# A hybrid RWKV-7 / Fourier layer on one core: four blocks normalised inside the scan, modulation weights loaded in another order, eight pairs of Fourier tiles

## The chip, the cores and the metric

The kernel runs on one core of a Trainium2 chip. The metric is the device time of one execution in microseconds; lower is better. Before the change the median of three runs is 3580.61 us (3576.83 to 3589.69).

## What is computed

One transformer-like layer over 2048 latent tokens of width 1024, with 256 context tokens ahead of them. In short (float32 throughout):

```
mod  = silu(c) @ w_ada + b_ada                  (shift, scale, gate; also for c_ctx)
h    = rmsnorm(x) * (1 + scale) + shift
p    = h @ w_in                                 (RWKV columns | Fourier columns | gates)
y_f, y_b = RWKV-7 scans of p over the tokens, forward and backward (context first)
o    = groupnorm_by_head(y_f + y_b) * lnx_g + lnx_b + bonus * v
r    = (o * (sigmoid(gd) @ g2)) @ w_up_r
f    = real(DFT over grid and channels) @ w_up_f
x1   = x + ga1 * ((sigmoid(gate_f) * f + sigmoid(gate_r) * r) @ w_out)
out  = rmsnorm(x1 + ga2 * swiglu(modulated rmsnorm(x1)))
```

## The kernel before

The work is in stages that follow one another. Large products are made of three single products of split operands (`hi*hi + hi*lo + lo*hi`, `mm3`, lines 251 to 253), 128x128 weights against 512 tokens.

**Modulation (lines 166 to 218).** Shift and scale of the first norm come from sixteen weight tiles of 512 KB: `wk` (line 197, TensorE products `modps` for the shift) and `wr` (line 190, VectorE products with `sB` and `sC`, the broadcast silu(c) and silu(c_ctx), summed into `mod`; `mod_j1` is the one for the context). `wk` and `wr` have three buffers each. `sB` and `sC` are loaded first. Then a loop over the eight k scales the first 512 latent tokens (`scaled`), and at once adds the shift and splits the result into `hh` and `hl` (`moved`), first for one half of the tokens, then for the other; three `mod_j1` stand in it. TensorE starts the first products of `w_in` (`pxps`, `fps`) on each k as it comes.

**Input projection (to about 1000 us)**, bound by TensorE.

**Scan (to 1776 us).** A loop over turns s from -2 to 17, each of 128 tokens in both directions. Its order is written out by hand: instructions given through the handles `PE, DV, AC, GP, SY` stay in program order on their queues. A turn inverts small triangular matrices on VectorE for the coming turns (`invert`), passes them through memory (`inv_store`, `merge_load`), merges their halves (`merge_a`: VectorE transposes `T` and TensorE `wps`; `merge_b`: VectorE `Wb`; `merge_c`: TensorE `t21ps`, ScalarE `TT`), and runs two links of the recurrence (`Chain`: `x`, `u`, `z`, `state`, `y`). At seven places in a turn `fill()` takes one step of a generator that supplies other work: first late gate columns, then `fourier()`. Its second part makes `fm = f @ w_up_f`: 32 steps of 12 products `pf`, 512 tokens in each `tb` (order 1, 2, 0, 3), against four pairs of tiles `fh`, `fl` loaded from memory (`load_f`). There are seven pairs in a ring: of the next `tb` three pairs are loaded ahead, the fourth when its buffer is free, at the first step of that `tb`. Once in a turn `ahead` loads weights `wf` and these tiles.

After `pf` the generator opens a pool for the group normalisation (`gn_open`, with the weights `g2`) and runs `gn_steps` for the four blocks of 128 tokens of the first `tb`. Each block goes through five steps: load of `y`, `yb`, `v` and the gate columns `sg`; sum of both directions, mean and centring (VectorE) and a square (ScalarE); variance, square root (ScalarE) and scaling; four transposes `gnt` (TensorE), four ScalarE evictions, addition of `v`; product `gng` with `g2` and multiplication. The `fill()`s of the loop are used up when this begins, so the blocks are worked off after the last turn.

**Merge and output product (1776 to about 2200 us).** `c_merge(n)` (lines 1135 to 1160) splits the four normalised blocks into `oh` and `ol`, makes `pr` (eight column tiles, 12 products each, weights `wr`), multiplies with the gates `gr` and adds `gf * fm`. These three operands of 256 KB for each column tile come from memory into a ring of eight buffers `t2`. For n > 0 `c_merge` normalises its own blocks (`gn_block`). Its instructions carry no fixed order: the compiler's planner places them. The order is merge 0, merge 1, output product `po` of 0, merge 2, and so on. `po` takes the weights `w_out` through `load_w`.

**Feed-forward (2200 us to the end)**, bound by TensorE.

## Time and profile before

| | |
|---|---|
| median of 3 runs | 3580.61 us |
| the profiled execution's own time | 3583.36 us |
| its span, first to last instruction | 3581.5 us |
| TensorE busy (products) | 3271.8 us, 91% |
| VectorE busy | 2405.0 us, 67% |
| ScalarE busy | 1560.3 us, 44% |
| GpSimd busy | 701.3 us, 20% |
| mean granted TensorE clock | 0.948 of full speed |

The span is the time from the first to the last instruction in the trace. Busy time is the time in which an engine had an instruction under way. The granted clock is the share of TensorE's full clock that it was given: 1.00 is 2.4 GHz, 0.50 is 1.2 GHz. A row of the timeline gives start and duration in us, engine, line (line 59 is the helper behind the handles of fixed order), operation, output and inputs, and in brackets how long the engine had been idle and what ended the wait. SPq is the queue of SyncE, which issues most transfers.

### The profile page before, as it was taken

The page shows a single profiled execution, that of the slowest core. Times are in us where ns is not written, and L with a number is a line of the kernel's source. Part 1 is how long each engine was busy: PE and PEld are TensorE (multiplying, and loading weights), DVE is VectorE, ACT ScalarE, POOL GpSimd, SP SyncE. Part 2 cuts the span into 40 slices and gives each one's busy share as a digit, 9 for nine tenths or more (in the row PEclk, how much of TensorE's full clock was granted, in tenths as well). Part 3 has the DMA queues.
Part 4 walks back from the last instruction along what each step waited for, and adds up shares of the span by engine and source line. Part 5 has one row for each costly group of instructions (what it writes and reads, how often), then busy time and mean ns, then how long its engine had stood idle before and what let it go on. Part 6 is the DMA issues. An engine that isn't in the chain of part 4 may idle for free.

```text
span 3581.5 us, 56320 instructions
## 1 busy us (share of the span) xinstructions
PE 3271.8 (91%) x20574; PEld 2700.2 (75%) x20574; DVE 2405.0 (67%) x4467; ACT 1560.3 (44%) x2910; POOL 701.3 (20%) x1099
## 2 busy tenths in 40 slices
PE   6999899999988887998758898999998999999997
PEld 5787777877877776777646686888877878888876
DVE  6677678757557777666376669777775387776354
ACT  3667556657543444434433335333353333333332
POOL 1143332322223333212132322000020000000000
PEclk9999999999999887999869998999999999999998
DMA  5354655545445556676677655222264432222453
GB/s 196 108 171 156 206 194 174 183 128 164 150 166 151 161 172 194 197 216 191 188 258 237 234 185 165 92 83 86 80 199 156 147 106 85 82 84 87 159 172 101
DMA packets 308436, 561.01 MB, mean 157 GB/s; under 512 B 91296, under 2 KB 102816, under 8 KB 308160
## 3 DMA queue, kind: packets, MB, share of 16 engines
q1 hardware_dynamic: 264256, 418.29, 36.4%
q0 software_dynamic: 43904, 139.12, 12.0%
q8 instruction: 163, 2.67, 0.3%
q14 instruction: 113, 0.93, 0.1%
HBM read 405.62 MB, written 151.66 MB: 156 GB/s over the span
## 4 chain that ended last, share of the span: by engine, by line
PE 36%; issue 10%; DVE 6%; DMA 6%; ACT 1%; POOL 1%; SPq 0%; DVEq 0%; POOLq 0%; ACTq 0%
PE pd L1352 12%; PE pT L251 2%; PE pT L252 2%; PE pT L253 2%; PE pf L59 2%; PE pB L251 2%; PE pB L252 2%; PE pB L253 2%; PE po L253 1%; PE po L251 1%; PE po L252 1%; PE xr L59 1%; DMA gr<-g_dr 1%; PE qk L59 1%; DMA wraw<-w_down 1%
## 5 line engine op out<-in xcount | busy, mean ns | idle before, releaser
L245 DVE TENSOR_TENSOR wlo<-wraw,whi 128x512 fp32r<-128x512 f32 x462 | 310.0, 695 | 378.3 <-ACT whi L244 365.6
L244 ACT ACTIVATE whi<-wraw 128x512 fp32r<-128x512 f32 x462 | 276.9, 626 | 483.9 <-PE pd L1352 192.7
L1352 PE MATMUL pd<-uh,whi 128*128 128x512 f32 x704 | 278.4, 396 | 23.1 <-ACT whi L244 21.5
L1352 PE MATMUL pd<-ul,whi 128*128 128x512 f32 x704 | 276.8, 393 | 0.0
L251 PE MATMUL pxps<-hh,whi 128*128 128x512 f32 (+2 forms) x720 | 252.1, 351 | 16.8 <-ACT hh L152 10.7
L1352 PE MATMUL pd<-uh,wlo 128*128 128x512 f32 x704 | 254.1, 391 | 0.7 <-DVE wlo L245 0.7
L251 PE MATMUL fps<-hh,whi 128*128 128x512 f32 (+1 forms) x688 | 249.2, 362 | 0.1
L252 PE MATMUL pxps<-hl,whi 128*128 128x512 f32 (+2 forms) x720 | 248.1, 346 | 0.0
L253 PE MATMUL pxps<-hh,wlo 128*128 128x512 f32 (+2 forms) x720 | 245.7, 346 | 2.4 <-DVE wlo L245 2.2
L253 PE MATMUL fps<-hh,wlo 128*128 128x512 f32 (+1 forms) x688 | 245.6, 357 | 1.4 <-DVE wlo L245 1.4
L252 PE MATMUL fps<-hl,whi 128*128 128x512 f32 (+1 forms) x688 | 243.6, 354 | 0.0
L1290 DVE TENSOR_TENSOR u<-u,pT 128x512 f32<-128x512 f32 x176 | 120.9, 687 | 142.0 <-PE pT L253 140.2
L1300 POOL DMA_DIRECT2D u_dr<-u x44 | 23.9, 544 | 838.5 <-DVE u L1299 792.3
L1352 PEld LDWEIGHTS pd<-uh,whi 128*128 128x128 f32 x704 | 133.9, 190 | 56.4 <-ACT whi L244 25.5
L59 DVE TENSOR_TENSOR tm<-Q,AI 128x126 f32<-128x126 f32 (+22 forms) x558 | 150.2, 269 | 29.5 <-DMA AI<-ab_dr 12.9
L59 DVE TENSOR_TENSOR Q<-Q,tm 128x126 f32<-128x126 f32 (+22 forms) x558 | 154.7, 277 | 20.2
L251 PEld LDWEIGHTS pxps<-hh,whi 128*128 128x128 f32 x720 | 138.0, 192 | 40.0 <-ACT hh L152 15.2
L1352 PEld LDWEIGHTS pd<-uh,wlo 128*128 128x128 f32 x704 | 132.7, 189 | 29.5 <-DVE wlo L245 1.6
L1352 PEld LDWEIGHTS pd<-ul,whi 128*128 128x128 f32 x704 | 134.1, 190 | 27.7
L252 PEld LDWEIGHTS pxps<-hl,whi 128*128 128x128 f32 x720 | 138.2, 192 | 20.6 <-issue 3.4
L253 PEld LDWEIGHTS pxps<-hh,wlo 128*128 128x128 f32 x720 | 138.0, 192 | 20.5 <-DVE wlo L245 3.8
L253 PEld LDWEIGHTS fps<-hh,wlo 128*128 128x128 f32 x688 | 130.4, 190 | 24.0 <-DVE wlo L245 3.0
(733 smaller groups left out, 8728.9 us busy)
## 6 DMA issues: line engine op xcount, KB each, us to landing
wraw<-w_in SPq DMA_DIRECT2D x210, 256.0 KB, 3.2
wraw<-w_down SPq DMA_DIRECT2D x176, 256.0 KB, 2.9
wA<-w_gu SPq DMA_DIRECT2D x176, 256.0 KB, 2.7
BD<-bd_dr SPq DMA_DIRECT2D x36, 512.0 KB, 6.7
KR<-kr_dr SPq DMA_DIRECT2D x36, 512.0 KB, 8.2
wada<-w_ada SPq DMA_DIRECT2D x32, 512.0 KB, 4.2
wraw<-w_out SPq DMA_DIRECT2D x64, 256.0 KB, 3.1
wf<-wf_dr SPq DMA_DIRECT2D x32, 512.0 KB, 6.8
```

The costliest lines, as they stand in the source:

```text
L59: return lambda *a, **k: tc.keep_in_program_order(f(*a, **k))
L244: nc.scalar.activation(out=hi[:, k0:k1, :], in_=raw, func=AF.Copy)
L245: nc.vector.tensor_tensor(out=lo[:, k0:k1, :], in0=raw, in1=hi[:, k0:k1, :].bitcast(F32), op=ALU.subtract)
L251: nc.tensor.matmul(ps, wh[:, k, :], xh(k), start=start and k == 0, stop=False)
L252: nc.tensor.matmul(ps, wh[:, k, :], xl(k), start=False, stop=False)
L253: nc.tensor.matmul(ps, wl[:, k, :], xh(k), start=False, stop=stop and k == K - 1)
L1290: nc.vector.tensor_tensor(out=o, in0=x, in1=y, op=ALU.add)
L1300: nc.gpsimd.dma_start(u_dr[f][:, TT[hf]:TT[hf] + 512], c)
L1352: nc.tensor.matmul(PD[ct], x[:, ct, :], y, start=f == 0 and i == 0, stop=f == FT - 1 and i == 2)
```

## The change

- **Modulation.** The order of the loads is now fixed: `wk` 0, `sB`, `wk` 1, `wr` 0, `wk` 2, `sC`, then `wr` and `wk` by turns. `wr` has five buffers, `wk` four. Silu of `sC` comes after the first `wr` product. The loop over k scales tile k for both halves, then moves and splits tile k - 1; it now holds five `mod_j1` instead of three.
- **Fourier tiles.** Eight pairs with a fixed slot each instead of a ring of seven; the eighth lies in the two `wraw` buffers. All four pairs of the next `tb` are loaded ahead.
- **Normalisation.** A second generator `gn_last` runs the four blocks of the first `tb` from turn 16 on: each `fill()` of the last two turns takes one of its steps ahead of the Fourier step. It uses tiles of the scan that are free by then (`QK0`, `BD`) and the banks `qk`. The result is stored to memory (`yb_dr`); `c_merge(0)` loads it into four `t2` buffers. The pool and `g2` for the other blocks are opened in `c_merge(1)`.

```
+        load_k(0)
+        SY.dma_start(sB, I["cc"][0:1, :].to_broadcast([128, D]))
+        load_k(1)
...
-            wr = wa.tile([128, D], F32, tag="wr", name=f"wadar{n}", bufs=3)
-            nc.sync.dma_start(wr, I["w_ada"][8 + n])
+            wr = wa.tile([128, D], F32, tag="wr", name=f"wadar{n}", bufs=5)
+            SY.dma_start(wr, I["w_ada"][8 + n])
+            if n < 6:
+                load_k(n + 2)
+            if n == 0:
+                SY.dma_start(sC, I["cc"][1:2, :].to_broadcast([128, D]))
...
-            if n < 5:
-                mod_j1(n)
+            if n == 0:
+                silu2(sC)
+            elif n < 4:
+                mod_j1(n - 1)
...
-        for k in range(KT):
+        for k in range(KT + 1):
             for m in range(2):
-                scaled(k, XS[m], RS[m], 0, DV)
-                moved(k, XS[m], 0, *[x[:, :, 256 * m:256 * m + 256] for x in H0[0]], DV)
-            if k in (3, 5, 7):
-                mod_j1(5 + (k - 3) // 2)
+                if k < KT:
+                    scaled(k, XS[m], RS[m], 0, DV)
+            for m in range(2):
+                if k:
+                    moved(k - 1, XS[m], 0, *[x[:, :, 256 * m:256 * m + 256] for x in H0[0]], DV)
+            if k > 3:
+                mod_j1(k - 1)
...
-                            FX[tb, k] = [fx.tile([128, 512], F32R, tag=f"f{y}", name=f"f{y}{tb}_{k}", bufs=7) for y in "hl"]
+                            if (4 * tb + k) % 8 == 7:
+                                FX[tb, k] = [wp.tile([128, 512], F32R, tag="wraw", name=f"f{y}{tb}_{k}", bufs=RW) for y in "hl"]
+                            else:
+                                FX[tb, k] = [fx.tile([128, 512], F32R, tag=f"f{y}{(4 * tb + k) % 8}", name=f"f{y}{tb}_{k}") for y in "hl"]
...
-                    load_f(i // 8 + 1, 3)
+                    load_f(i // 8 + 1, 4)
...
+        def gn_last():
...
+            for j in (0, 1):
+                next(B[j])
+            yield
+            for p in range(2):
+                for k in range(4):
+                    for j in (2 * p, 2 * p + 1):
+                        next(B[j])
+                    if k == 3:
+                        for j in (2 * p, 2 * p + 1):
+                            SY.dma_start(yb_dr[128 * j:128 * j + 128, :], YB[4 * TB[0] + j])
+                            if p == 0:
+                                next(B[j + 2])
+                    yield
...
-        def fill():
+        def fill(extra=True):
+            if extra and GL:
+                next(GL[0], None)
             return next(src[0], 0) is None
...
+            if s == NS - 2:
+                GL.append(gn_last())
             fill()
             ch.u()
             fill()
...
+        if n == 1:
+            GN.clear()
+            gn_open(gps.enter_context(tc.tile_pool(name="gnp", bufs=1)))
         for i in range(4):
-            yb = YB[4 * tb + i] if n == 0 else gn_block(4 * tb + i)
+            if n:
+                yb = gn_block(4 * tb + i)
+            else:
+                yb = t2("yb0")
+                nc.sync.dma_start(yb, yb_dr[128 * i:128 * i + 128, :])
```

## Rows read from the trace of the kernel before

**Rows 1.** Stretches: from:to, us, busy PE, PEld, DVE, ACT, POOL (count), clock, DMA share, GB/s.
```profile
0.00:45.00 45.00, 23.43 (x107) 22.85 (x107) 26.63 (x39) 13.23 (x13) 13.79 (x14) 1.00 0.92 316
50.00:75.00 25.00, 15.97 (x45) 9.83 (x45) 18.52 (x48) 7.42 (x16) 0.00 (x0) 0.90 0.00 0
60.00:400.00 340.00, 321.28 (x1517) 253.71 (x1517) 250.79 (x443) 232.89 (x426) 105.33 (x186) 0.97 0.47 155
...
1728.00:1755.00 27.00, 26.83 (x379) 21.88 (x379) 7.35 (x18) 13.19 (x33) 4.79 (x8) 0.92 0.51 137
...
1776.00:1830.00 54.00, 15.07 (x59) 12.35 (x60) 31.27 (x60) 15.63 (x37) 12.94 (x9) 0.51 0.75 248
1830.00:1902.00 72.00, 55.00 (x235) 45.21 (x234) 56.62 (x88) 21.53 (x46) 32.02 (x22) 0.82 0.79 266
```

**Rows 2.** Timeline of the first 81 us: start, duration.
```profile
19.30 10.37 PE L59 MATMUL modps<-sc,wadak 128*128 128x2 f32 x48 [19.30 <-DMA wadak<-w_ada]
...
50.45 1.16 DVE L59 SCALAR_TENSOR_TENSOR wada<-wadar,sB 128x1024 f32<-128x1024 f32 x1
...
52.55 0.48 DVE L59 SCALAR_TENSOR_TENSOR xs<-xs,gsc,rs 128x256 f32<-128x256 f32 x1
...
60.00 0.51 ACT L152 ACTIVATE hh<-xs,mod 128x256 fp32r<-128x256 f32 x1 [0.95 <-DVE xs L59]
...
80.86 0.40 PE L253 MATMUL fps<-hh,wlo 128*128 128x512 f32 x1
...
82.38 3.25 DVE L148 SCALAR_TENSOR_TENSOR xs<-xs,gsc,rs 128x256 f32<-128x256 f32 x8
```

**Rows 3.** Transfers of the first 50 us.
```profile
DMA packets 7553, 14.74 MB, mean 295 GB/s; under 512 B 2560, under 2 KB 3840, under 8 KB 7552
```

**Rows 4.** Waits of TensorE, 1430 to 1776 us: total, times, longest.
```profile
PE pf L59 <- DMA wf<-wf_dr: 12.2, 4, 4.4
PE pf L59 <- DMA fh<-fth_dr: 9.1, 3, 6.9
```

**Rows 5.** Timeline of the last two turns and the first merge product.
```profile
1739.41 1.62 POOL L59 DMA_DIRECT2D tb_dr<-Q  x2 [0.99 <-DMA UV<-v_dr]
...
1746.84 1.43 DVE L59 STREAM_TRANSPOSE T<-TT 32x512 f32<-32x512 f32 x2
...
1753.70 1.29 DVE L59 TENSOR_TENSOR Wb<-wps,cn 128x512 f32<-128x512 f32 x2 [5.43 <-PE wps L59]
...
1774.35 1.32 ACT L59 ACTIVATE Y<-xr 64x256 f32<-64x256 f32 x4 [1.32 <-PE xr L59]
...
1830.11 1.82 PE L251 MATMUL pr<-oh,wr 128*128 128x512 f32 x4
```

**Rows 6.** Groups by line, 1776 to 1830 us: busy us, mean ns, idle before.
```profile
L59 PE MATMUL gng<-sg,g 128*128 128x128 f32 x32 | 8.3, 441 | 6.0 <-ACT gnb L59 3.3 <-DVE gnb L59 2.7
...
L59 ACT ACTIVATE gnb<-gnt,vec 128x128 f32<-128x128 f32 x16 | 6.0, 456 | 3.1 <-PE gnt L59 3.1
L59 DVE TENSOR_TENSOR gny<-gny,s 128x512 f32<-128x512 f32 x8 | 5.9, 743 | 0.3
...
L59 ACT ACT_TABLE_LOAD x1 | 1.3, 1283 | 0.0
```

**Rows 7.** Transfers, 1776 to 1902 us: issues, KB each, us to landing.
```profile
DMA packets 16937, 32.56 MB, mean 258 GB/s; under 512 B 1704, under 2 KB 2984, under 8 KB 16932
...
gnb<-y_dr SPq DMA_DIRECT2D x12, 256.0 KB, 4.4
```

**Rows 8.** Stretches as in rows 1, with the transfer engines hardly idle.
```profile
1776.00:1806.00 30.00, 6.35 (x24) 4.99 (x24) 12.08 (x22) 7.23 (x15) 10.18 (x7) 0.51 0.97 327
...
1796.00:1806.00 10.00, 4.15 (x16) 3.56 (x16) 3.57 (x5) 2.13 (x5) 1.17 (x1) 0.50 1.05 387
...
1836.00:1866.00 30.00, 20.90 (x99) 17.25 (x97) 24.70 (x36) 9.20 (x19) 17.85 (x12) 0.88 0.96 347
```

**Rows 9.** Products pr, 1776 to 1906 us: ns min/median/max, first and last start.
```profile
L253 PE MATMUL pr<-oh,wr x64: 389/389/628, 1832.0 to 1902.0; 128*128 128x512 f32 x64
```

More of the change, by code (lines that the diff above doesn't have):

```diff
@@ L174, in layer_kernel, with load_k, silu2 @@
                                 scalar1=0.5, scalar2=None, op0=ALU.mult)
+        WK = []
+        def load_k(n):
+            wk = wa.tile([128, KT, 128], F32, tag="wk", name=f"wadak{n}", bufs=4)
+            SY.dma_start(wk, I["w_ada0"][n])
+            WK.append(wk)
+        load_k(0)
+        SY.dma_start(sB, I["cc"][0:1, :].to_broadcast([128, D]))
+        load_k(1)
         sC = wa.tile([128, D], F32, name="sC")
-        nc.sync.dma_start(sC, I["cc"][1:2, :].to_broadcast([128, D]))
         tB = wa.tile([128, D], F32, name="tB")
-        for s_ in (sB, sC):
+        def silu2(s_):
             nc.scalar.activation(out=tB, in_=s_, func=AF.Tanh, scale=0.5)
-            nc.vector.scalar_tensor_tensor(out=s_, in0=tB, scalar=1.0, in1=s_, op0=ALU.add, op1=ALU.mult)
+            DV.scalar_tensor_tensor(out=s_, in0=tB, scalar=1.0, in1=s_, op0=ALU.add, op1=ALU.mult)
+        silu2(sB)
         mps = pmm.tile([128, 512], F32, tag="mm", name="modps")
@@ L560, in b8, with gn_steps @@
         return x.unsqueeze(2).to_broadcast([128, 8, 64])
-    def gn_steps(i, E, bank):
+    def gn_steps(i, E, bank, tiles=None):
         sy, dv, ac, pe = E
-        y, yb, v_ = [GN[0].tile([128, 512], F32, tag=n, name=n, bufs=4 if n == "gnb" else 2) for n in ("gny", "gnb", "gnv")]
+        y, yb, v_, sg, s8 = tiles or [GN[0].tile(f, F32, tag=n, name=n, bufs=b) for n, f, b in (
+            ("gny", [128, 512], 2), ("gnb", [128, 512], 4), ("gnv", [128, 512], 2), ("sg", [128, 128], 2), ("s8", [128, 2, 8], 3))]
         sy.dma_start(y, y_dr[0][128 * i:128 * i + 128, :])
@@ L568, in gn_steps @@
         sy.dma_start(v_, bv_dr[i].rearrange("p t s -> p (t s)"))
-        sg = GN[0].tile([128, 128], F32, tag="sg", name="sg", bufs=2)
         sy.dma_start(sg, sg_dr[:, CTX + 128 * i:CTX + 128 * i + 128])
         yield
-        s8 = GN[0].tile([128, 2, 8], F32, tag="s8", name="s8", bufs=3)
         dv.tensor_tensor(out=y, in0=y, in1=yb, op=ALU.add)
@@ L1015, in fourier @@
                 flush()
-            gn_open(gps.enter_context(tc.tile_pool(name="gnp", bufs=1)))
-            i0 = 4 * TB[0]
-            B = [gn_steps(i0 + j, (SY, DV, AC, PE), lambda n: pfl.tile([128, 512], F32, tag="fl", name=n)) for j in range(4)]
+            for _ in range(4):
+                yield
+        def gn_last():
+            T = []
+            for j in range(2):
+                q = sp.tile([128, 2, 2, 4, 128], F32, tag="QK0", name=f"gq{j}", bufs=2).rearrange("p a b c d -> p (a b c d)")
+                T.append([q[:, 512 * m:512 * m + 512] for m in range(4)])
+            g2 = T[0][3]
+            SY.dma_start(g2, I["g2"])
+            GN.extend((None, g2))
+            st_ = T[1][3]
+            BDt = [sp.tile([128, 4, 2, 2, 64], F32, tag="BD", name=f"gb{j}", bufs=4).rearrange("p a b c d -> p (a b c d)") for j in range(4)]
+            B = []
+            for j in range(4):
+                sg, s8 = st_[:, 128 * (j % 2):128 * (j % 2) + 128], st_[:, 256 + 16 * j:272 + 16 * j].rearrange("p (a b) -> p a b", b=8)
+                y, yb, v_ = T[j][0:3] if j < 2 else (BDt[2 * j - 4][:, 0:512], BDt[2 * j - 4][:, 512:1024], BDt[2 * j - 3][:, 0:512])
+                B.append(gn_steps(4 * TB[0] + j, (SY, DV, AC, PE), lambda n: pqk.tile([128, 512], F32, tag="qk", name=n), (y, yb, v_, sg, s8)))
             for j in (0, 1):
@@ L1021, in fourier @@
             yield
-            yield
-            for k in range(8):
-                if k == 3:
-                    for j in (2, 3):
+            for p in range(2):
+                for k in range(4):
+                    for j in (2 * p, 2 * p + 1):
                         next(B[j])
-                for j in range(2):
-                    next(B[2 * (k // 4) + j])
+                    if k == 3:
[3 more added lines that the diff above has]
+                                next(B[j + 2])
                     yield
         ahead = [None]
-        def fill():
+        def fill(extra=True):
+            if extra and GL:
+                next(GL[0], None)
             return next(src[0], 0) is None
+        GL = []
         JA = 16
@@ L1044, in layer_kernel @@
             if s == 0:
-                while fill():
+                while fill(False):
                     pass
@@ L1104, in layer_kernel @@
             pass
+        for _ in GL[0]:
+            pass
     pcs.close()
```

5 lines of the change are left out of this document (2 added, 3 removed).

## The prediction

> **What bounds the kernel now.** I read the stretches first: how busy each engine is, the granted clock and the transfer rate. The projection is a TensorE stage (321 of 340 us), so whatever comes earlier ahead of it arrives in full at its end [rows 1]. Three places are not bound by TensorE. Up to 45 us the transfers run at 0.92 of their engines' time while TensorE waits for weights; from 50 to 75 us nothing is transferred, and TensorE waits for `hh` and `hl` [rows 1, 2]. In the Fourier steps it waits 9.1 us for `fh` [rows 4]. And between the last eviction of the scan, which ends at 1775.7 us, and the first `pr` at 1830.1 us lie 54.4 us [rows 5], in which TensorE is busy for 15 us at a clock of 0.51, that is 1.2 GHz [rows 1]. Behind that, up to the last `pr` at 1902 us [rows 9], it has 55 of 72 us. From there on the stages are TensorE's again. The change works at just these places.
>
> **Modulation.** `wk` 0 takes the place of `sB` at the head of the queue, so TensorE starts earlier. But its work is not the limit: 48 instructions take 10.4 us, so the 128 take 28 us [rows 2], and the same bytes have to come. 14.74 MB come in the first 50 us [rows 3]; about 1 MB of `w_in` may come after the last `wr`, which leaves 13.7 MB, at 316 GB/s [rows 1] 43.4 us. Then one product (1.2 us) and, as now between the last product and the first `scaled`, some 0.9 us: 45.5 instead of 52.6 us [rows 2]. **Gain 7 us.** Ends: 0, if the transfers are simply full and the order does not matter, and 13, if the planner also puts the third `xs` and the rest of `w_in` (2.6 MB, 8 us) behind the `wr`.
>
> The loop takes 52.55 to 81.3 us [rows 2], since ScalarE's copy waits for `scaled`, and VectorE for the copy (0.95 us idle before each copy). With the copy a tile behind, VectorE has no such gaps: 32 instructions at 3.25/8 = 0.41 us and five `mod_j1` at 1.2 us, as the product beside them [rows 2], 19 us; with the last products of TensorE 21.5. **Gain 7 us**; ends 4 (two more `mod_j1` in the way, TensorE at 1.2 GHz) and 9. Both together 14, bounds 4 and 22. Nothing hides it, and nothing gives it back, as the projection follows.
>
> **Fourier tiles.** The fourth pair is loaded a turn ahead, so 9.1 us of waits go [rows 4]. Late next is `wf`, at 12.2 us in four waits [rows 4], which the change leaves alone; and in turns where VectorE's inversion is close behind, some of the gain goes to it. **Gain 7 us**, bounds 3 and 12 (more than the wait, because after 6.9 us of it TensorE runs at half clock for a while). The same number of transfers is issued on SyncE, only earlier; the two `wraw` buffers have no other user until `w_out`, whose loads begin after the last `pf`.
>
> **Normalisation in the last two turns.** It leaves the stretch behind the scan; what does it cost inside? A block is seven 512-wide VectorE instructions at some 0.72 us and four small ones, about 5.5 us; on ScalarE four evictions of 0.46, a square and a root, 2.7 us; on TensorE transposes and eight `gng` passes at 0.44 us (half clock) [rows 6], 2.3 us at full clock. In sum that is 22, 11 and 9 us in two turns, 1728 to 1775.7 us, of which the first has 7.4 us of VectorE and 13.2 of ScalarE in 27 [rows 1]: there is room on both. Not the sum costs, but the order of the queues. I followed the steps through the two turns from today's times; the times below are estimates from them:
>
> - Loads of the first pair wait for nothing and land by 1728 us; step 1 runs while VectorE is idle. Cost 0.
> - Step 2, variance and root, stands on VectorE ahead of the last columns of `invert`. Two blocks take 4.3 us, and ScalarE's first root needs a table, 1.3 us [rows 6]. So `tb_dr`, issued at 1739.4 [rows 5], goes some 5.4 us later; `T` had little more than that in hand.
> - Step 3's additions stand ahead of `state`, 3.7 us, and so ahead of the next `x`.
> - Step 4 multiplies, then SyncE stores `yb` (waiting for VectorE) and loads the second pair. Behind this wait on SyncE stand two `wf` and the first `wr`; they are not needed at once. The loads go out at about 1754 and land 4.4 us later [rows 7], the second block's two later.
> - The second pair's step 1 stands on VectorE **ahead of** `T` in turn 16. It waits for those loads and works 4.5 us, so `T` comes at 1763 instead of 1746.8 [rows 5], and TensorE, with `wps` next in line, stands still for about 6 us.
> - Its step 2 stands ahead of `Wb`: 1769 instead of 1753.7 [rows 5]. Then `t21ps`, `TT`, and behind `TT` on ScalarE the evictions of step 3, 3 us, ahead of `UV`. The chain's `pu` and `z` are then 17 us late, and the last `Y` with them.
>
> So the scan ends **17 us later**, at 1792.7; bounds 5 (the loads land earlier and the planner's waits are loose) and 30 (TensorE falls to 1.2 GHz in these turns as well).
>
> On the table load a rule speaks against the change. The Trainium skill, "ScalarE: Activation LUTs", What ACT_TABLE_LOAD costs, adds a drain to the load and gives 2.66 us for every switch of sets. By the page the scan would be 1.4 us later than by the row.
>
> **Merges.** The first `pr` now needs four reloads: 4.4 us to landing [rows 7], 0.8 MB more at 327 GB/s [rows 8] 2.4 us, and a split, about 9 us with the start. That would be 1802. But it is not this that decides: the operands do. From 1776 to 1902 us 32.56 MB came [rows 7]. The loads of four blocks (3.4 MB) leave, 1.05 MB of reloads come: 30.2 MB. The rate is 327 and 347 GB/s where the transfers hardly pause [rows 8], 258 on average [rows 7], 387 at best [rows 8]. I take 337, since the pauses came from waits for the blocks' normalisation: 89.6 us. With 2 us to start, the merges end at 1792.7 + 91.6 = 1884.3 instead of 1902. **Gain 18 us net of the delay**; bounds: minus 10 (258 GB/s, 117 us) and plus 41 (delay 5 us, 78 us at 387 GB/s). VectorE has 31 + 57 us there [rows 1] and loses 22; it would not bound. The store of `yb` has 20 us before the scan's end and hides there; without that cover it would be some 5 us on the reload.
>
> A transfer's price by the Trainium skill ("DMA: Bandwidth & Descriptors", Anatomy of one DMA): about 2.0 us plus bytes over 436 GB/s, for the four reloads 4.4 us. By that the first `pr` would come 2.4 us sooner; the end of the merges stays.
>
> **Sum.** 14 + 7 + 18 = 39 us off the profiled execution's 3583.4, 3544.4. It stands 2.8 us above the median, so the forecast against the median is 3542.
>
> **Rivals.**
> - *Forecast*: 3542, own range 3525 to 3560. Chance 0.50.
> - *The new order of the modulation loads does nothing*, because the transfers at 0.92 bound it whatever comes first [rows 1]: 7 us less, 3549. Chance 0.07.
> - *Steps fit between the chain's links, transfers run at their best.* Delay 5, merges 41, start 20, tiles 10: 71 us, 3510. For it: VectorE waits long stretches in these turns, 5.4 us before `Wb` alone [rows 5]. Against it: the order of `T` behind the second pair. Chance 0.25.
> - *The merges are bound by transfers at 258 GB/s*, because eight `t2` buffers, four of them with `yb`, allow no more in flight. Then the 18 us become minus 10: 14 + 7 - 10 = 11 us, 3570. Against it: the rates of rows 8, with the same eight buffers. Chance 0.13.
> - *Slower: the chain of the last two turns stops at each step.* Each of nine steps holds VectorE, ScalarE or TensorE for what it waits for. Today the four blocks with their loads take the 54 us; if the chain stands still for them all and TensorE falls to 1.2 GHz, so that turn 16's 27 us of work [rows 1] double, the delay is 81 us. From 56 us the whole change is worth nothing (1775.7 + 56 + 91.6 is 1902 + 21), from 74 it is slower by over 0.5%; at 81 it loses 46 in the merges, wins 21, and gives 3606. Against it: the first pair's steps find their inputs ready. Chance 0.05.
>
> **How the numbers follow.** A measurement of this kernel can tell about 0.5% from no change, 18 us: 3562.7 to 3598.5. Faster: forecast, order does nothing, best fit, and a sixth of the fourth case, 0.84; the same 0.11; slower 0.05. The range 3502 to 3570 leaves out some 0.06 below and, above, half of the 258 GB/s case and the slower one: under 0.2.
>
> **What would show it.** First `scaled` at about 45 us and 20 us of loop; no `pf` waiting for `fh` or `fl` after the first `tb`; in turn 16 VectorE idle before the second pair's `gny` by a transfer, TensorE idle before `wps` by some 6 us; one table load in turn 16; first `pr` some 9 us after the last `Y`; the last `pr` of merge 1 near 1863 us at 330 to 350 GB/s. I am wrong if the last `Y` comes before 1760 or after 1785, if the merges run at 260 GB/s, or if the start gains under 4 us.

## The result and the profile after

| | before | after |
|---|---|---|
| median of the timed runs, us | 3585.15 (3576.83 to 3592.51, 4 runs) | 3540.76 (3529.67 to 3548.12, 4 runs) |
| profiled execution, us | 3583.36 | 3548.12 |
| its span, us | 3581.5 | 3546.3 |

The ratio is 0.9874, with a 95% interval of 0.9837 to 0.9912. The change makes the kernel 1.3% faster, and 3540.8 us stands 1.2 us from the forecast of 3542. That closeness is partly luck: the gain forecast was 39 us and the medians show 44.4, and the four executions after the change spread over 18 us. The profiled execution after the change was the slowest of its four, so the pair of traces shows 35.2 us of difference.

**Where the time went.** I took the start of the same instruction in both traces, at the places where one stage hands over to the next. "Gain" is how much earlier it starts after the change:

```
                                         before    after    gain   forecast, to here
first scaled                              52.55    48.86     3.7     7
37th scaled (start and loop done)         212.2    196.5    15.7    14
first gate product gps (projection done) 1007.4   1000.2     7.2    14
first t21ps of turn 16                   1725.1   1712.8    12.2    21
last xr (the scan's last product)        1774.2   1784.4   -10.2     4
first pr (merges begin)                  1830.1   1801.3    28.8
last pr of merge 1                       1902.0   1871.9    30.1    39
last po (output products done)           2172.8   2132.4    40.4    39
end of the span                          3581.5   3546.3    35.2    39
```

The two ends agree, but not each stage: 8.5 us of the start are lost again in the projection, the last two turns take 5 us more than forecast, the merges win that back, and 10 us came from a stage that I had not named. Between the last `po` and the end 5.2 us are lost once more, in the feed-forward, which the change does not touch: it takes 1413.9 us here, 1408.7 in the kernel before, and 1406.4 to 1412.8 in the twelve kernels below. I count these 5.2 us as scatter; their cause was not looked for.

The stretches of the kernel after the change answer to [rows 1, 8], in the same columns (us, busy time and count of PE, PEld, DVE, ACT, POOL, granted clock, DMA share, GB/s):

```profile
0.00:45.00 45.00, 29.05 (x129) 28.01 (x130) 25.24 (x39) 13.82 (x15) 14.43 (x14) 1.00 0.90 316
60.00:150.00 90.00, 84.91 (x420) 69.26 (x419) 60.81 (x112) 56.92 (x104) 14.03 (x48) 0.98 0.43 132
1712.00:1786.00 74.00, 60.22 (x740) 50.43 (x738) 34.45 (x76) 34.21 (x86) 6.31 (x11) 0.82 0.51 156
1786.00:1802.00 16.00, 0.73 (x2) 0.64 (x3) 7.59 (x15) 3.44 (x7) 1.46 (x3) 0.58 0.90 317
1802.00:1872.00 70.00, 59.24 (x264) 48.67 (x262) 59.34 (x92) 23.76 (x52) 41.41 (x27) 0.85 1.02 368
1786.00:1872.00 86.00, 59.97 (x264) 49.31 (x264) 66.93 (x106) 27.20 (x59) 42.86 (x29) 0.80 1.00 358
```

The 54 us that stood between the scan and the merges, with TensorE at half clock [rows 1], have become 15. From 1786 to 1872 us the transfer engines have no pause: share 1.00 at 358 GB/s, where the same stage had 0.75 and 0.79 before [rows 1]. So I read the stage after the change as bound by transfers; no run here loads less in it, so this reading is not tested.

The start, in the timeline of the kernel after (start, duration, engine, line, operation; in brackets the idle time before it and what ended it):

```profile
14.75 0.38 SPq L114 DMA_DIRECT2D xs<-xT  x1
16.14 4.57 SPq L136 DMA_DIRECT2D xe<-xT  x1
20.76 4.27 SPq L261 DMA_DIRECT2D wraw<-w_in  x2
...
25.62 1.76 SPq L59 DMA_DIRECT2D wadak<-w_ada  x1
...
31.12 10.40 PE L59 MATMUL modps<-sc,wadak 128*128 128x2 f32 x48 [3.14 <-DMA wadak<-w_ada]
...
37.20 0.33 SPq L59 DMA_DIRECT2D wadar<-w_ada  x1
...
43.28 0.42 DVE L59 TENSOR_SCALAR rs<-rmsps 128x256 f32<-128x256 f32 x1
...
43.95 1.29 DVE L263 TENSOR_TENSOR wlo<-wraw,whi 128x512 fp32r<-128x512 f32 x2
45.16 1.75 DVE L59 RECIPROCAL rs<-rs 128x256 f32<-128x256 f32 x1
...
46.84 1.21 DVE L59 SCALAR_TENSOR_TENSOR wada<-wadar,sB 128x1024 f32<-128x1024 f32 x1
...
48.86 1.67 DVE L59 SCALAR_TENSOR_TENSOR xs<-xs,gsc,rs 128x256 f32<-128x256 f32 x4
```

The modulation weights come first among themselves, but the planner put an x block, the edge columns and two projection weights ahead of the fifth of them on SP. TensorE stands before the last 64 products, and these then take until 45.8 us. The last `wr` leaves SP at 37.20 us and lands 6.6 us later, at 43.8. Its product on VectorE begins only at 46.84, since VectorE is busy until then with `rs` of the second half of the tokens and with the split of two projection weights. Then `scaled` runs four in a row; in the kernel before VectorE stood still for ScalarE's copy ahead of nearly every `hl`, as here:

```profile
59.09 0.48 DVE L59 SCALAR_TENSOR_TENSOR hl<-xs,mod,hh 128x256 fp32r<-128x256 f32 x1 [0.58 <-ACT hh L152]
```

The last two turns in the same view, against [rows 5]:

```profile
1725.37 1.28 ACT L59 ACT_TABLE_LOAD   x1
...
1742.84 0.92 SPq L59 DMA_DIRECT2D gb<-y_dr  x2
...
1748.62 0.69 DVE L59 TENSOR_TENSOR gb<-gb 128x512 f32<-128x512 f32 x1 [9.50 <-DMA gb<-y_dr]
...
1753.76 1.43 DVE L59 STREAM_TRANSPOSE T<-TT 32x512 f32<-32x512 f32 x2
...
1759.23 1.28 DVE L59 TENSOR_TENSOR Wb<-wps,cn 128x512 f32<-128x512 f32 x2
...
1784.59 1.32 ACT L59 ACTIVATE Y<-xr 64x256 f32<-64x256 f32 x4 [1.32 <-PE xr L59]
...
1789.67 0.42 SPq L585 DMA_DIRECT2D gny<-y_dr  x1
...
1793.79 1.74 SPq L1194 DMA_DIRECT2D yb<-yb_dr  x4
...
1801.27 2.08 PE L269 MATMUL pr<-oh,wr 128*128 128x512 f32 x4 [16.67 <-DMA gr<-g_dr]
```

VectorE idles 9.5 us for the second pair's loads with `T` behind them in its queue. And the reload of `yb` leaves SP only at 1793.8, behind the eight loads of the next two blocks (the first at 1789.7). Ahead of these stands the load of `g`, for which SP waits 5.1 us until a store of `fm` has landed (waits of SP, 1783 to 1794 us):

```profile
SPq L626 <- DMA fm_dr<-ev: 5.1, 1, 5.1
```

The row of the first `pr` names `gr`, which this product does not read; its weight load waits 16.8 us for the split `oh` of the reloaded blocks.

TensorE's waits from 1418 to 1786 us, against [rows 4] (total us, times, longest):

```profile
PE pf L59 <- DMA wf<-wf_dr: 14.2, 4, 5.3
PE wps L59 <- DVE T L59: 11.6, 5, 10.4
```

No wait for `fh` or `fl` is left, `wf` is about what it was (14.2 us, 12.2 before), and the long wait of `wps` is new.

### The profile page after: what moved, and what is told of

It is laid out like the page before. It is cut to its first block, busy times and chain, and to the rows that moved or that the text cites. A ratio compares the mean times of both kernels' runs of the same rounds, so it can differ in the third digit from the quotient of the medians.

```text
span 3546.3 us, 56317 instructions
## 1 busy us (share of the span) xinstructions
PE 3263.2 (92%) x20574; PEld 2692.1 (76%) x20574; DVE 2409.7 (68%) x4467; ACT 1555.2 (44%) x2910; POOL 699.7 (20%) x1099
## 4 chain that ended last, share of the span: by engine, by line
PE 34%; issue 11%; DMA 7%; DVE 7%; ACT 1%; POOL 1%; SPq 1%; DVEq 0%; POOLq 0%; ACTq 0%
PE pd L1405 12%; PE pT L269 3%; PE pT L270 3%; PE pT L271 3%; PE pB L269 2%; PE pB L270 2%; PE pB L271 2%; PE pf L59 2%; PE xr L59 1%; DMA gr<-g_dr 1%; PE po L271 1%; PE po L269 1%; PE po L270 1%; PE qk L59 1%; DVE wlo L263 1%
## 5 line engine op out<-in xcount | busy, mean ns | idle before, releaser
L269 PE MATMUL pxps<-hh,whi 128*128 128x512 f32 (+2 forms) x720 | 251.7, 350 | 10.6 <-ACT whi L262 8.2
L269 PEld LDWEIGHTS pxps<-hh,whi 128*128 128x128 f32 x720 | 138.6, 193 | 31.3 <-ACT whi L262 10.6
L269 PEld LDWEIGHTS fps<-hh,whi 128*128 128x128 f32 x688 | 129.9, 189 | 22.4 <-issue 3.1
```

The lines of the kernel that those rows point to most:

```text
L269: nc.tensor.matmul(ps, wh[:, k, :], xh(k), start=start and k == 0, stop=False)
```

## The experiments

All gains below are against the profiled execution of the kernel before, at the places of the table above. Two measures depend little on what happened earlier: A, the time from the first `t21ps` of turn 16 to the last `po`; and B, the part of it up to the first `pr`. In the kernel before A is 447.8 and B 105.1 us; after the change 419.6 and 88.5.

**The three parts alone.** My theory was that each part acts where the prediction puts it: the start by about 14 us, the tiles by 7, the normalisation by 18. The rival was that they share a bound, so that a part alone gives another sum.

The modulation part alone (the hunks of `load_k`, `silu2` and the two-stage loop):

```
+        load_k(0)
+        SY.dma_start(sB, I["cc"][0:1, :].to_broadcast([128, D]))
+        load_k(1)
...
-        for k in range(KT):
+        for k in range(KT + 1):
```

> The kernel before with the modulation part of the change alone. My theory: the head start of some 15 us at the 150th microsecond comes from this part alone, and about half of it is lost between 320 and 750 us because the planner gives the projection another order when its beginning comes earlier; so the first late gate product (gps) starts 7 us earlier than before (1000 instead of 1007) and the span is 7 to 9 us shorter. Rival 1: the loss comes from elsewhere in the change, then gps starts 15 us earlier. Rival 2: the part gains nothing, and the earlier end of the projection is run-to-run spread, then gps starts within 2 us of 1007.

Measured: median 3574.6 (8 runs) to 3580.0 for the kernel before, ratio 0.9984 (0.9956 to 1.0012). The interval includes no change at all. In the trace it has 3.6 us at the first `scaled`, 15.2 at 212 us, 9.5 at the first gate product and 6.4 at the end. So it wins its 15 us at once and does not keep them.

The Fourier tiles alone:

```
+                            if (4 * tb + k) % 8 == 7:
+                                FX[tb, k] = [wp.tile([128, 512], F32R, tag="wraw", name=f"f{y}{tb}_{k}", bufs=RW) for y in "hl"]
...
-                    load_f(i // 8 + 1, 3)
+                    load_f(i // 8 + 1, 4)
```

> The kernel before with the eight pairs of Fourier tiles alone. My theory: TensorE's 9 us of waits for fh and fl after the first products go, wf waits stay at 12 to 14 us, and part of the gain is taken by waits for VectorE's state: the last y product of the scan starts 3 to 7 us earlier than 1774, first pr as much earlier. Rival: the waits only move to wf, then the wf waits rise to over 18 us and the scan ends within 1 us of 1774.

Measured: 3571.7 in one run; 0.3 us at the first gate product, 10.5 at turn 16, 11.6 at the end. The last `xr` comes 10.6 us earlier, more than the 3 to 7 that I expected. The products `pf` wait there for `wf` alone (TensorE's waits, 1420 to 1766 us):

```profile
PE pf L59 <- DMA wf<-wf_dr: 12.1, 3, 4.1
```

The normalisation alone (`gn_steps` with tiles given, `gn_last`, `fill`, and the merge's reload):

```
+            if s == NS - 2:
+                GL.append(gn_last())
...
+                yb = t2("yb0")
+                nc.sync.dma_start(yb, yb_dr[128 * i:128 * i + 128, :])
```

> The kernel before with the normalisation in the last two turns alone (Fourier tiles still in a ring of seven). My theory: the scan ends about 22 us later than before (last y product at about 1796), because the second pair's first step holds VectorE's transposes T and TensorE waits about 10 us before wps; the merges then take about 86 us from the scan's end to the last pr of the second merge, bound by transfers at 350 to 370 GB/s, instead of 126; last pr at about 1884 instead of 1902; span 18 to 24 us shorter. Rival: the merges gain from the other parts, then last pr stays within 5 us of 1902.

Measured: median 3549.8 (3 runs), ratio 0.9916 (0.9856 to 0.9976), A 419.8 and B 86.2 us. So A and the delay are this part's alone: the last `xr` stands at -12.7 against the kernel before, the last `pr` of merge 1 at +27.6, the last `po` at +35.0. From the last `Y` to the last `pr` of merge 1 it takes 85.9 us, 86 expected; the delay of the scan on its own clock is 19.8 us, some 22 expected.

By the timed medians the three parts give 5.5, 8.3 (one run) and 30.2 us, 44 together; the whole change gives 44.4. They add up as far as such medians can tell (one of the three is a single run, and the start's gain is within its noise), and nothing points to a shared bound.

**Loads and loop apart.** The head start of 15 us is the loads' and the loop's together. With the loads in the new order and depth, but the old loop with five `mod_j1`:

```
-            if k in (3, 5, 7):
-                mod_j1(5 + (k - 3) // 2)
+            if k > 2:
+                mod_j1(k)
```

> The kernel before with the new order and depth of the modulation loads alone; the loop over k is as before, with five instead of three of the context products in it. My theory (order of the planner): the first scaled tile comes 4 us earlier (48.9 instead of 52.6), the loop takes 2 us longer than before, head start some 2 us at 150 us; whether this is kept to the end of the projection depends on the order the planner finds, so the change of the head start between 150 and 1000 us is anything from minus 10 to plus 5. Rival (the loss belongs to the stage: some work there is bound by transfers and catches up): a small head start is not lost, or in proportion, about half of it.

Measured: 3582.7; 4.7 us at the first `scaled`, 7.6 at 212 us, 9.4 at the first gate product, 0.6 at the end (it is gone again in the scan; the cause stays open). I had expected 2 us at the 150th microsecond.

With the two-stage loop and the old loads (three `mod_j1` in it):

```
-            if k in (3, 5, 7):
-                mod_j1(5 + (k - 3) // 2)
...
+            if k > 5:
+                mod_j1(k - 1)
```

> The kernel before with the loop over k in two stages alone (scale tile k, then move and split tile k - 1); loads as before, three context products in the loop. Theory: the first scaled tile stays at 52.6, the loop takes 18 us instead of 28.7, head start about 10 us at 150 us. If the later loss is the planner's order, the head start at the end of the projection need not be half of that; if it belongs to the stage, about half, 5 us, is left at the first gps.

Measured: 3575.6 (the kernel before on that chip 3571.4, one run each); -0.2 at the first `scaled`, 10.1 at the 19th, 14.1 at 212 us, but 7.8 at the first gate product. So the loop is the larger half of the head start, not an equal one. The stretch from 60 to 150 us of the kernel before, the loads alone and the loop alone says why it is more than the gaps in the loop:

```profile
60.00:150.00 90.00, 78.95 (x355) 61.50 (x355) 52.74 (x100) 48.43 (x91) 11.20 (x41) 0.91 0.37 111
60.00:150.00 90.00, 79.80 (x386) 63.58 (x387) 59.98 (x111) 52.18 (x97) 12.69 (x44) 0.94 0.39 119
60.00:150.00 90.00, 86.28 (x425) 70.65 (x425) 62.18 (x118) 56.95 (x105) 13.39 (x47) 0.98 0.43 127
```

In the kernel before TensorE waits for `hh` five times behind the loop's copies. It idles 11.1 of these 90 us at a granted clock of 0.91; with the loop alone it idles 3.7 us, and the clock is 0.98.

**Where the head start goes.** Six kernels with the whole new start (after, the start alone, and the four below that leave the projection alone) have 14.3 to 16.5 us at 212 us and 6.3 to 14.1, mean 9.0, at the first gate product. Up to 320 us nothing is lost. In the kernel after, 5.5 of the 8.5 us that go are gone where the kernel before stands at 467 us; the other 3 were not followed up. From 340 us on the transfers of the turn to the second token part come closer together. Stretches of the kernel before and of the kernel after; the same work lies some 16 us earlier in the second:

```profile
360.00:380.00 20.00, 17.98 (x92) 14.09 (x92) 20.00 (x39) 15.56 (x32) 18.25 (x16) 0.99 0.64 211
380.00:400.00 20.00, 15.69 (x82) 12.86 (x81) 13.80 (x25) 11.38 (x23) 7.37 (x14) 1.00 0.78 292
```

```profile
360.00:380.00 20.00, 16.80 (x94) 13.92 (x95) 14.36 (x27) 10.95 (x22) 8.73 (x15) 1.00 0.92 342
```

ScalarE waits there for a projection weight, and TensorE for ScalarE's split of it; the timeline and the waits of TensorE of the kernel after, 320 to 460 us:

```profile
376.30 1.30 ACT L262 ACTIVATE whi<-wraw 128x512 fp32r<-128x512 f32 x2 [5.25 <-DMA wraw<-w_in]
```

```profile
PE pxps L269 <- ACT whi L262: 3.9, 2, 3.2
```

These 3.9 us are a quarter of TensorE's idle time from 320 to 460 us, 16.4 us in all, to 12.2 in the kernel before; the rest are short waits for ScalarE and VectorE, most of them in the Fourier products. Among the transfers are the later modulation rows, 512 KB each, with nobody waiting for them so early. So I moved them three weight columns back:

```
-                    for jt in range(16 + 2 * ci + min(ci, 2), 18 + 2 * ci + min(ci + 1, 2)):
+                    for jt in range(16 + 8 * max(ci - 3, 0) // 3, 16 + 8 * max(ci - 2, 0) // 3):
```

> The changed kernel with the 32 loads of the later modulation rows (512 KB each) begun at the fourth weight column of the second token part instead of the first, so that they lie outside the stretch at 360 to 376 us where the transfers ran at 350 to 430 GB/s and a weight split waited 5.25 us for its load. Theory (the head start is given back where the transfers are full at the turn to the second part): TensorE's idle time between 320 and 460 us falls from 16.4 us to 12 or less, and the gain over the kernel before at the 53rd projection eviction (447 us in the kernel before) rises from 12.6 to 15 or more. Rival (it is given back by the order of the instructions, whichever transfers there are): idle stays at 15 to 17, the gain there at 11 to 13. The moved loads themselves may cost up to 3 us further on, where the columns now carry two to three of them each.

Measured: 3534.9 in one run; idle time 12.4 us, gain 17.7 us at the 53rd eviction and 16.6 at the first gate product, 9.4 more than the kernel after. The stretch in this kernel:

```profile
360.00:380.00 20.00, 17.64 (x101) 15.09 (x99) 13.20 (x24) 11.58 (x24) 8.49 (x15) 1.00 0.76 254
```

The theory holds for the 53rd eviction of `pxps`, where no kernel with the rows in their old place has over 13.1; the kernel with three edits below, with the rows moved too, has 18.7 there and 12.7 us of idle time. At the first gate product one with the old place has 14.1 and the one with three edits 12.2, so there the 16.6 of a single run proves less. How the rows act is not shown: TensorE's waits for `whi` fall only from 3.9 to 3.3 us, and most of the idle time saved lies in the other short waits. The edit moves the VectorE products of the rows with their loads; which of the two counts was not taken apart.

The other way round, the start can be made earlier still, with the x block and the edge bound behind the modulation weights:

```
-XS.append(load_x(0, nc.sync))
+XS.append(load_x(0, SY))
...
-        nc.sync.dma_start(xe, XTv[:, :, c0:c0 + 2])
+        (SY if c0 == 768 else nc.sync).dma_start(xe, XTv[:, :, c0:c0 + 2])
```

> The changed kernel with the loads of the first context x block and of the edge columns bound to SP's order behind the modulation weights. In the changed kernel the wk 4 load left SP only at 25.62 us, behind the x block (14.75), the edge (16.14 and 25.07) and a projection weight (20.76), and the first scaled began at 48.86. Theory (SP's queue order held the weights back): wk 4 leaves SP by about 20 us, TensorE's last modulation weights end near 40 and the first scaled begins at 43 to 45. Rival (the transfers are full, at 316 GB/s in this stretch, so what is put ahead of one load is behind another): first scaled unchanged at 48 to 49.5, or the context block late afterwards, so that the 18th scaled gains nothing. Both expect that little of it is left at the first gate tile (1000.2 us in the changed kernel): within 3 us.

Measured: 3544.3; the timeline of TensorE and of VectorE:

```profile
26.86 10.24 PE L59 MATMUL modps<-sc,wadak 128*128 128x2 f32 x48
...
37.95 3.41 PE L59 MATMUL modps<-sc,wadak 128*128 128x2 f32 x16
```

```profile
43.35 1.67 DVE L59 SCALAR_TENSOR_TENSOR xs<-xs,gsc,rs 128x256 f32<-128x256 f32 x4
```

TensorE has its weights without a wait at 26.9 us and the first `scaled` comes at 43.35, 5.5 us earlier. So what stands ahead of the weights on SP held the start back. It does not follow that the transfer engines had room. Two stretches of the kernel after, and the same of this one:

```profile
9.00:39.00 30.00, 23.05 (x103) 22.19 (x104) 18.47 (x22) 10.47 (x9) 12.11 (x6) 1.00 1.02 367
25.00:30.00 5.00, 2.97 (x11) 2.25 (x11) 5.00 (x6) 0.27 (x1) 3.47 (x2) 1.00 1.03 247
...
9.00:39.00 30.00, 26.94 (x122) 26.53 (x122) 21.59 (x28) 10.15 (x11) 11.46 (x6) 1.00 1.03 392
25.00:30.00 5.00, 5.00 (x23) 4.82 (x23) 5.00 (x8) 1.53 (x2) 1.78 (x1) 1.00 1.03 412
```

The engines are full in both, but at another rate. Up to the landing of the last `wr`, at 43.8 and 39.1 us, 14.2 MB are moved in either kernel; of the packets 2528 are under 512 B in the kernel after and 1038 here, where the edge columns come later. At 154 us, though, the gain is 11.3 instead of 15.9, and at the first gate product 10.6: what is put behind the weights is late later.

**The wait of `wps`.** Theory: the second pair's loads are issued too late, since they share the gates' buffer with the first pair and stand behind its store on SP. With the second pair's gates in a place of their own its loads can go out early in turn 16, three steps sooner (1708 us, 3 us after the `t21ps` of that turn; in the kernel after 30 us after it):

```
-                sg, s8 = st_[:, 128 * (j % 2):128 * (j % 2) + 128], st_[:, 256 + 16 * j:272 + 16 * j].rearrange("p (a b) -> p a b", b=8)
+                sg, s8 = st_[:, 128 * j:128 * j + 128] if j < 2 else BDt[2 * j - 3][:, 512:640], st_[:, 256 + 16 * j:272 + 16 * j].rearrange("p (a b) -> p a b", b=8)
...
-                            if p == 0:
-                                next(B[j + 2])
...
                         next(B[j])
+                        if p + k == 0:
+                            next(B[j + 2])
```

> The changed kernel with the loads of the second pair of blocks three steps earlier (at the second step of turn 16 instead of the fifth, with gate columns in a place of their own). My theory: VectorE no longer waits 9.5 us for the transfer of the second pair; T comes some 7 us earlier, TensorE's wait before wps falls from 10.4 to 2 to 4 us, and the scan takes 6 to 8 us less from t21ps of turn 16 to the last y product (70.7 us now, 63 to 65 then). Rival: VectorE's own work ahead of T (4.5 us) and ScalarE's evictions are what holds the chain, then the scan's end moves by under 3 us.

The rival remedy leaves the loads where they are and puts two empty steps between the pairs, so that `T` goes ahead of the second pair:

```
             for p in range(2):
+                for _ in range(2 * p):
+                    yield
                 for k in range(4):
```

> The changed kernel with two empty steps between the two pairs of blocks, so that the second pair's first step comes in turn 17 behind T and Wb instead of ahead of them. My theory: T and Wb come within 8 us of their old distance from t21ps of turn 16 (T at 22 us, now 41), TensorE's wait before wps falls below 3 us, and from t21ps of turn 16 to the last y product it takes 55 to 60 us instead of 70.7; the merges, bound by transfers, start as much earlier and end 10 to 14 us earlier. Rival 1: the second pair then holds the chain of turn 17 by as much (state and UV behind its steps), then 66 us or more. Rival 2: the store of the second pair comes so late that its reload holds the first pr, then pr starts no earlier.

Measured: 3522.7 and 3530.0 (the kernel before 3571.4, one run each); B is 77.0 and 77.8 us instead of 88.5. The early loads, in the timelines of VectorE and of TensorE:

```profile
1732.01 0.68 DVE L59 TENSOR_TENSOR gb<-gb 128x512 f32<-128x512 f32 x1
...
1736.52 1.43 DVE L59 STREAM_TRANSPOSE T<-TT 32x512 f32<-32x512 f32 x2
```

```profile
1737.26 0.48 PE L59 MATMUL wps<-T,LT 32*128 32x128 f32 x2 [0.18 <-DVE T L59]
```

VectorE has no idle time before the second pair, `T` follows at once, and TensorE's wait of 10.4 us is 0.2. From `t21ps` of turn 16 to the last `xr` it takes 61.1 us instead of 71.6, more of a gain than the 6 to 8 that I expected. So 10 of the 22.5 us of delay are this one wait; the other 12 were not taken apart. Empty steps do nearly the same: 62.1 us, where I had expected 55 to 60, so 13 us of delay are left. A is 408.9 with the early loads and 414.8 with the empty steps, 419.6 with neither.

**The output products.** Here the change gave 10.3 us that I had not forecast. The normalisation alone gives 7.4 of it (last `pr` of merge 1 to last `po`: 270.9 before, 263.4), the other parts alone between -1.1 and 1.2. TensorE's waits from 1902 to 2175 us in the kernel before show what went:

```profile
PE gnt L587 <- DVE s L582: 12.8, 1, 12.8
PE gnt L587 <- DVE gny L583: 9.9, 1, 9.9
```

These belong to the later blocks' normalisations. In the kernel before, one of their loads left SP behind ten loads of `w_out`:

```profile
1920.12 19.82 SPq L243 DMA_DIRECT2D wraw<-w_out  x10
...
1948.53 0.43 SPq L566 DMA_DIRECT2D gny<-y_dr  x1
```

Neither wait is left with the normalisation alone. That they went because all that is ahead of them is earlier is argued; why the planner orders these loads otherwise was not examined. In the kernel after, from 1870 to 2140 us, others stand in the list:

```profile
PE pr L269 <- DVE gr L1209: 9.6, 4, 3.6
PE po L271 <- DVE wlo L263: 5.8, 7, 1.6
```

`po` waits for its weights, and the x loads of 2 MB, issued during the merges, take 13.5 us. I cut these in eight, so that they could move out of the merges:

```
-        nc.sync.dma_start(x1, XTv[:, :, CTX + 512 * tb:CTX + 512 * tb + 512])
         for ct in range(8):
+            nc.sync.dma_start(x1[:, ct, :], XTv[:, ct, CTX + 512 * tb:CTX + 512 * tb + 512])
```

> The changed kernel with the load of x for the output product (two loads of 2 MB that the planner puts at the beginning of the merges) cut in eight, each beside its column tile, so that they can come when transfers have room. My theory: the merges are bound by transfers (368 GB/s, share 1.02), so 4 MB less in their 86 us let the last pr of the second merge come 5 to 11 us earlier. Rival: the operands' chain through GpSimd and VectorE bounds them, then within 2 us of 1872.

Measured: 3527.5. The gain that I expected, the last `pr` of merge 1 earlier by 5 to 11 us, did not come: from the last `Y` it takes 89.3 us instead of 86.0. But the theory was not tested by it, since the planner left all sixteen loads, 4 MB, in this stretch (1771.6 to 1860.9 us of this kernel), with 31.0 MB in all instead of 30.8:

```profile
x<-xT SPq DMA_DIRECT2D x16, 256.0 KB, 6.1
```

So whether the merges would end earlier with less to load, or are held by the chain of their operands through GpSimd and VectorE, stays open. The gain is behind them: from the last `pr` of merge 1 to the last `po` 252.9 us instead of 260.5, and `po` waits for `wlo` 1.4 us instead of 5.8:

```profile
PE po L271 <- DVE wlo L263: 1.4, 4, 0.5
```

The three kernels with the cut load have 252.9 to 257.8 us there, the six with the new normalisation and without it 257.4 to 263.4. A gains 5.2 (414.4). The rest of this run's lead lies ahead of turn 16, where the edit changes nothing: a single run of this kernel is good to some 10 us, the measures A and B to some three or four (A is 419.6, 419.8, 422.2 and 416.6, and B 88.5, 86.2, 89.7 and 84.4 in the four kernels with the new normalisation and none of these edits).

**Two and three edits together.** The early loads (three steps sooner, the same edit as above) and the cut x load together, then with the moved modulation rows as well:

> The changed kernel with both edits that helped in single looks: the second pair's normalisation loads two steps earlier (with a buffer of their own for the gates), and the x load of the output products cut in eight. Theory (the two act in different stretches, one before 1790 us, one behind 1870): from the step-16 t21 product to the first pr 77 us (88.5 in the changed kernel), from the last pr of merge 1 to the last po 253 us (260.5), together some 18 us less than the changed kernel's median of 3540.8: 3518 to 3528, ratio to the kernel before 0.982 to 0.986. Rival (the earlier scan end only brings the merges' loads forward into the same full transfers): the first pr comes earlier, but from there to the last po it takes longer by as much, and the time is 3530 or more.

> The changed kernel with the three edits that kept what they won in their stretches: the second pair's loads two steps earlier, the x load of the output products cut in eight, and the modulation rows begun at the fourth column. Theory (three stretches that don't touch): the gain over the kernel before at the last projection eviction is 14 to 17 us (6.3 with the first two edits alone), the step from the t21 product of step 16 to the first pr 75 to 77 us, and the time some 7 us under that of the two edits alone (3526.3): 3514 to 3524, ratio 0.980 to 0.985. Rival (a gain in the projection is lost again in the scan, which waits for its own loads): the ratio is that of the two edits, 0.982 with the same interval, and the time 3524 to 3532.

Measured: with two edits median 3526.3 (4 runs), ratio 0.9822 (0.9780 to 0.9863), B 74.8 and A 400.9 us. With three 3520.3 (5 runs), ratio 0.9841 (0.9815 to 0.9867), B 78.7 and A 408.1, and 12.2 us at the first gate product instead of 6.3. Both have lower medians than the change (3540.8), by 14 and 20 us, but were timed beside other runs of the kernel before, and the intervals of the ratios touch that of the change. So both are faster than the kernel before, and that they beat the change is likely but not shown. Which of the two is better can't be told: 6 us in the medians speak for three edits, the ratios for two, and A differs by 7 us between them although the third edit lies ahead of it. With the three, the gain at the first gate product is under the expected 14 to 17, and 4.6 us go again between 607 and 754 us.

## Why the prediction was right

By stages in the pair of traces, gain against forecast: start and projection 7.2 against 14, scan to turn 16 5.0 against 7, last turns and merges 17.9 against 18, output products 10.3 against nothing, feed-forward a loss of 5.2 against nothing; 35.2 against 39. The third term, the largest, fits, and the second lies in its range; for the rest the total came out by errors that cancel.

**Modulation, loads: half the size.** Forecast 7 us, measured 3.7 (4.7 alone), under the 4 at which I had said I would be wrong. The transfers came as forecast: the last `wr` landed at 43.8 us, 43.4 forecast. The step that failed is what stands behind it, "Then one product (1.2 us)" and some 0.9 us. The 1.2 and the 0.9 us are there, but the product begins 3.1 us after the landing, since VectorE has `rs` and a weight's split ahead of it. In the kernel before this gap could have been read, too: `wr` landed at 45.8 us and its product began at 50.45 [rows 2]. TensorE's products, held up by SP's order (the fifth weight left at 25.62 us), end at 45.8 us; with 0.9 us behind them the first `scaled` would have come at 46.7, so they decide 1.2 of the 3.4 us at most. In the kernel with the x block behind the weights the gap is 2.6 us.

**Loop: too small.** Forecast 7, measured 8.0 up to the 19th `scaled` and 4.2 more up to 154 us. The loop itself takes 20.5 us, 21.5 forecast. What I left out is the stretch behind it: from 60 to 150 us TensorE idles 5.1 us instead of 11.1, with fewer stops for `hh`, and its granted clock is 0.98 instead of 0.91.

**"Whatever comes earlier arrives in full at its end" failed.** The two together were 15.7 us where 14 were forecast, and 7.2 arrived (9.0 as the mean of six kernels). I read "321 of 340 us" as bound by TensorE. Of the other 19 us 11 lie up to 150 us, in the loop's wake, and 8 beyond 320 us, at the turn to the second token part, where the idle time grows as the stretch moves earlier: 16.4 us from 320 to 460, 12.2 before. With the moved rows it was 12.4 us.

**Fourier tiles: in the range.** Forecast 7 (3 to 12): 10.2 us alone from the first gate product to turn 16, 5.0 within the whole change, and -9.7 to 6.8 in kernels without this part. The size is within the scatter of the scan; the mechanism, no `fh` or `fl` wait left, is shown.

**The last two turns: right step, too small.** The forecast had `T` at 1763, `Wb` at 1769, 6 us of `wps` and 17 in all. On the clock of the kernel before (12.2 us later than that of the kernel after at turn 16) they came at 1766.0 and 1771.4; `wps` waited 10.4 and the delay is 22.5 us. The loads went out as forecast, at 1755.0 on that clock instead of 1754, but took 5.8 us (1742.84 to 1748.62) instead of 4.4, and the second block's came 2.9 us later instead of two. From `Wb` on `Y` loses 5 us more, at a granted clock of 0.82 in these turns. The last `Y` ends at 1785.9 us, 0.9 past the bound at which I had said I would be wrong, though 12.2 us had been gained ahead of turn 16. There was one table load, of 1.28 us: it began 0.02 us after `Y` ended, and the root began 0.13 us after it. So the 2.66 us of the Trainium skill ("ScalarE: Activation LUTs", What ACT_TABLE_LOAD costs) do not appear here.

**Merges: right in sum.** Forecast 91.6 us from the last `Y` to the end of merge 1 and 18 net of the delay; measured 86.0 (1785.9 to 1871.9) and 17.9. The transfers of these 86 us:

```profile
DMA packets 15691, 30.82 MB, mean 358 GB/s; under 512 B 1563, under 2 KB 2575, under 8 KB 15687
```

I had 30.2 MB at 337 GB/s. So the merges were 5.6 us shorter and the delay 5.5 us longer than I had them, and the net came out right partly by luck. The first `pr` comes 15.4 us after the last `Y` has ended, not 9: I had the reloads at the head of SP's queue, where `g` with its wait of 5.1 us and eight loads of the next blocks stand. From the first issue of the reloads to the last landing it takes 6.3 us, near my 6.8. The other price in the prediction, 4.4 us for all four, is too low here; the section it names is on transfers that GpSimd issues, and these go out on SyncE. The late first `pr` did not set the end of the merges as far as the full transfers show.

**What was missing: the output products.** 10.3 us, in a stage that I had put at nothing: "From there on the stages are TensorE's again." Two waits, of 12.8 and 9.9 us, lay behind the merges and went with the normalisation. The loss in the projection and the gain in the output products nearly cancel.

**The rivals.** That the order of the loads does nothing falls: the same transfers in another order gave up to 9.2 us. That the merges run at 258 GB/s falls by the 358 above; the eight buffers do not hold them. The best fit, with a delay of 5 us, is not what the change does; the early loads bring the delay to 12 us. The chain did not stop at each of nine steps: the long wait in it is one, of 10.4 us, and it is late by 22.5 us.

## What to carry to other kernels

A head start can be lost at the next place that is bound by something else: look at the fullest stretch of transfers behind it and at the waits in it, not only at the busy share of the stage. And when a load has landed, look at what its consumer's queue still holds ahead of it. When work is moved into another stage's gaps, the cost is what stands behind its waits in the engine's queue; loads issued earlier took that away. When a late stage is made earlier, look past its end for waits that may go with it.

## What the runs showed that I had not expected

Single executions of one kernel differ by up to 31 us (3563.4 to 3594.3 for the kernel before, on one chip). Little of this seems to arise from turn 16 to the last `po`, where five kernels with the old normalisation lie between 445.7 and 448.0 us; where it arises was not measured on two traces of one kernel. Measures between two instructions are far sharper than the whole time.

The transfers ran at 368 GB/s with no pause for 70 us, in single slices of 2 us at up to 411, and at 392 over 30 us of the start in the kernel with the x block behind the weights; my 337 from [rows 8] was what a stretch with pauses gives.
